# A two-layer decoder on one core: negated scores with a running minimum, one operation to mix two maps, and the gate row applied to the projection's banks

## The chip, the cores and the metric

The kernel runs on one core of a Trainium2 chip. Its engines are TensorE (PE, with its weight loads PEld), VectorE (DVE), ScalarE (ACT), GpSimd (POOL) and SyncE (SP, which issues most of the transfers). They run beside each other and wait for each other by semaphores. The metric is the device time of one execution in microseconds (us); lower is better.

## The reference

The reference is a decoder trunk of two layers on 512 tokens of 1024 channels, in float32. Cut to what matters:

```python
for l in range(2):
    sh1, sc1, g1, sh2, sc2, g2 = split(silu(c) @ w_ada[l] + b_ada[l], 6)
    h = rms(x, norm1[l]) * (1 + sc1) + sh1
    y = mlstm_mixer(h) if l == 0 else diff_attention(h)   # both end in ... @ w_out
    x = x + g1 * y
    h = rms(x, norm2[l]) * (1 + sc2) + sh2
    x = x + g2 * grouped_moe(h)        # 16 experts, 2 of 1 group of 4 for each token

def diff_attention(h):                 # 8 heads, 2 maps each, head dim 64
    q, k, v = h @ w_in                 # q, k: rms with a gain, partial rotation
    for each block of 128 queries, each head:
        sc = (q * 64**-0.5) @ k.T      # two maps c = 0, 1, causal
        p = softmax(where(mask, sc, -inf))
        o = (p[0] - lam * p[1]) @ v
    return (rms(o) * (1 - lam_init)) @ w_out
```

So the gate row `g1` (1024 values, one for each output channel) multiplies the output of the mixer's last projection.

## The kernel before

The program goes through layer 0's mixer (to about 282 us), its MoE (308 to 575), layer 1's attention (575 to 918) and its MoE (943 to the end). Between mixer and MoE lies the routing: RMS norm of each tile of 128 tokens, transposes (`x2T`, line 1075), router matmuls (`psr`, line 1087), choice and places of tokens on DVE, and an indirect transfer that gathers the tokens of each expert (`xg`, line 1311). Most matmuls of weights are done in three terms: a weight tile is split by `split` into a part `h` (ACT copy, line 228) and a remainder `l` (DVE subtraction, line 229), and `triple` (line 237) multiplies h·h, l·h and h·l.

The order on each engine is set by a scheduler that plays a timeline; a queue `later`/`step` in the kernel delays pieces of work by some steps, `ordered` keeps an instruction at its place in program order, and `tc.issue_after` holds the instructions under it behind another instruction. Tiles in PSUM come from pools of 4 (`mm`), 2 (`y`) and 2 (`t`) buffers.

**out_proj** (line 486) is the last projection of both mixers. It runs in two halves of two token tiles (t = 0, 1, then t = 2, 3); each token tile has two banks `po` of 512 columns. In half 0 the eight weight tiles `wo` (128x1024) are loaded and split, and POOL then multiplies each `wo` by the gate row `grow` in place (line 512). So half 0 needs the gate on its banks (DVE, line 499) before they are added to `x` (DVE, line 500), while half 1 splits the tiles already multiplied and only adds. The names `wos0hk` stand for layer 0, half h, weight tile k; `guse00`, `guse01` are the first tiles of the MoE's weights, split early.

**scores** (line 908) makes the two maps of a block j and a head h. For each map a matmul gives `s`, one DVE operation adds the mask row and takes the running maximum (line 920, a custom operation plus a read of its accumulator), line 923 multiplies the maximum by -0.125, and ACT takes the exponent with scale 0.125 and that bias. Then the reciprocal of the sums (line 927), the factor of map 1 (line 928), map 1 times the factor (line 929) and map 0 plus that (line 930). In `attention_constants` the column `wcq` holds the gain of q, which ACT applies when it copies the turned q (line 904).

**normed_T** (line 370) does the norm of a token tile at the start of a layer. Its `rstd_of` is a DVE operation (line 366) and a power on POOL (line 367); for t = 2, 3 of layer 1 it comes close to the last additions of layer 0's MoE (line 1616).

Of the kernel before, what the change touches and what calls it, by code (L numbers as in the profile page):

```python
# [60 lines left out]
def trunk(ctx, tc, x, c, positions, norm1, norm2, w_ada, b_ada, a_w_in, a_b_if, a_h_norm, a_w_out,  # L61
# [151 lines left out]

    loads, last, act_last = [], [], []

# [154 lines left out]
    def normed_T(l, t, pool, junk, dst, rows, bank):  # L370

        ss = small.tile([P, 1], F32, tag="ss", name=f"ss{l}{t}", bufs=4)
        A.activation(junk, xt[t], AF.Square, accum_out=ss)
        r = rstd_of(ss, 1, D, f"r{l}{t}")
        ps = [bank(f"hT{l}{t}{hf}") for hf in range(2)]
# [110 lines left out]
    def out_proj(l, half, grow, h, turned, w_out, kept, mods, done):  # L486
# [4 lines left out]
        def products(t, kt):  # L491
            while (t, kt) not in turned:
                run_first()
            triple(ps[t, 0], ps[t, 1], *(p[:, kt] for p in tokens(h, t)), *parts[kt], kt == 0, kt == NK - 1)
            if kt == NK - 1:
                for n in range(2):
                    cols = slice(n * 512, (n + 1) * 512)
                    if half == 0:
                        V.tensor_tensor(ps[t, n], ps[t, n], grow[:, cols], op=ALU.mult)
                    V.tensor_tensor(xt[t][:, cols], xt[t][:, cols], ps[t, n], op=ALU.add)  # L500
                done(t)
            step()

        for ch in range(4):
# [3 lines left out]
            for k in range(2):  # L508
                kt = ch * 2 + k
                parts[kt] = split(raw[:, k:k + 1], 1, D, f"wos{l}{half}{kt}")  # L510
                if half == 0:
                    G.tensor_tensor(raw[:, k], raw[:, k], grow, op=ALU.mult)  # L512
                if kt < NK - 3:
                    for t in ts:
                        products(t, kt)
                if k:
                    next(mods, None)
# [292 lines left out]
    def attention_constants(pool):  # L810
# [17 lines left out]
        for nm, w in (("q", b_q_norm), ("k", b_k_norm)):  # L828
# [6 lines left out]
            for c0 in (0, BHD):  # L835
                SP.dma_start(wc[c0 + R2:c0 + BHD], w[0:1, R2:].rearrange("o d -> d o"))
            tab = const.tile([P, NT, 2 * R2], F32, name=f"tab{nm}")
            bc = lambda a: a[:, None, :].to_broadcast([P, NT, ROPE_HALF])
# [9 lines left out]
    def attention(outer, mods):  # L848
# [4 lines left out]
        with ExitStack() as st:  # L853
# [12 lines left out]
            past(maskW[:, S - P:])  # L866
            V.tensor_scalar(maskW[:, S - P:], maskW[:, S - P:], 0.0, NEG, op0=ALU.is_gt, op1=ALU.mult)
            a1 = scale_of(1, slice(0, 4)) + scale_of(1, slice(4, 8))
# [39 lines left out]
            def scores(j, h):  # L908
# [5 lines left out]
                for cc in range(2):  # L914
# [4 lines left out]
                    p = pool.tile([P, S], F32, tag=f"p{cc}", name=f"p{j}{h}{cc}", bufs=3)  # L919
                    V.tensor_tensor_reduce(p[:, 0:n], ps[:, 0:n], maskW[:, S - n:S], scale=1.0, scalar=NEG,  # L920
                                           op0=ALU.add, op1=ALU.max, accum_out=mx[:, cc:cc + 1])
                    pr.append(p)
                    V.tensor_scalar(mx[:, cc:cc + 1], mx[:, cc:cc + 1], -0.125, None, op0=ALU.mult)  # L923
                    A.activation(p[:, 0:n], p[:, 0:n], AF.Exp, scale=0.125, bias=mx[:, cc:cc + 1],  # L924
                                 accum_out=mx[:, 2 + cc:3 + cc])
                p0, p1 = pr
                V.reciprocal(mx[:, 4:6], mx[:, 2:4])
                V.scalar_tensor_tensor(mx[:, 5:6], mx[:, 5:6], mx[:, 2:3], nlam, op0=ALU.mult, op1=ALU.mult)
                V.tensor_scalar(p1[:, 0:n], p1[:, 0:n], mx[:, 5:6], None, op0=ALU.mult)
                V.tensor_tensor(p0[:, 0:n], p0[:, 0:n], p1[:, 0:n], op=ALU.add)  # L930
                later(5, lambda: probs_T(j, h, p0, mx))
# [371 lines left out]
    def moe(l, pool, grow, fetch, by_rank, xgs, lst, lstd, ids, gates, rows2, twins, count, exc, past, pk, eid):  # L1303
# [269 lines left out]
        for e in range(NE):  # L1573
# [32 lines left out]
            if e == NE - 1:  # L1606
                mine = weighted_few(py, e), mine
                for t in range(NT):
# [5 lines left out]
                    for hf in range(2):  # L1614
                        x = xt[t][:, hf * 512:(hf + 1) * 512]
                        V.tensor_tensor(x, x, banks[t][hf], op=ALU.add)
            elif e >= NE - NSEL:
# [93 lines left out]
```

## Time and profile before

| | |
|---|---|
| median of 3 runs | 1228.6 us (1227.84 to 1230.41) |
| profiled execution, own time | 1225.23 us |
| its span, mean TensorE clock | 1223.4 us, 0.952 |
| PE busy | 1126.9 us (92%) |
| DVE busy | 808.9 us (66%) |
| ACT busy | 659.1 us (54%) |
| POOL busy | 307.7 us (25%) |

The span is the time from the first to the last instruction of the profiled execution. The busy shares are means over stages that have different limits. Where a row gives a clock, 1.00 is 2.4 GHz and 0.50 is 1.2 GHz; values between are means over a stretch that saw both.

### The profile page before, as it was taken

The page shows a single profiled execution, that of the slowest core. Times are in us where ns is not written, and L with a number is a line of the kernel's source. Part 1 is how long each engine was busy: PE and PEld are TensorE (multiplying, and loading weights), DVE is VectorE, ACT ScalarE, POOL GpSimd, SP SyncE. Part 2 cuts the span into 40 slices and gives each one's busy share as a digit, 9 for nine tenths or more (in the row PEclk, how much of TensorE's full clock was granted, in tenths as well). Part 3 has the DMA queues.
Part 4 walks back from the last instruction along what each step waited for, and adds up shares of the span by engine and source line. Part 5 has one row for each costly group of instructions (what it writes and reads, how often), then busy time and mean ns, then how long its engine had stood idle before and what let it go on. Part 6 is the DMA issues. An engine that isn't in the chain of part 4 may idle for free.

```text
span 1223.4 us, 17320 instructions
## 1 busy us (share of the span) xinstructions
PE 1126.9 (92%) x5954; PEld 816.0 (67%) x5954; DVE 808.9 (66%) x1617; ACT 659.1 (54%) x1118; POOL 307.7 (25%) x245
## 2 busy tenths in 40 slices
PE   5999999988999999996899999978797999999976
PEld 3677777777787875332897877757586787774322
DVE  4566878887888995006856566675677899893024
ACT  3456675443788885112655555555553888883110
POOL 2555482462211111101211021223233211111100
PEclk8999999997999999998999999988896999999998
DMA  9788662195799999999124444411275899999994
GB/s 345 267 284 302 230 216 104 59 346 194 280 383 382 386 380 368 398 408 370 37 70 141 138 169 138 173 69 74 99 280 193 316 386 385 377 380 372 396 414 182
DMA packets 104172, 320.81 MB, mean 262 GB/s; under 512 B 12673, under 2 KB 25097, under 8 KB 103056
## 3 DMA queue, kind: packets, MB, share of 16 engines
q1 hardware_dynamic: 95120, 298.67, 65.8%
q0 software_dynamic: 8960, 20.99, 4.7%
q8 instruction: 49, 0.80, 0.3%
q14 instruction: 43, 0.35, 0.1%
HBM read 309.66 MB, written 20.97 MB: 270 GB/s over the span
## 4 chain that ended last, share of the span: by engine, by line
PE 70%; DMA 12%; DVE 11%; ACT 4%; issue 2%; POOL 1%; SPq 0%; DVEq 0%; POOLq 0%; ACTq 0%
PE pge L237 8%; PE pue L237 8%; PE pge L1339 6%; PE po L237 6%; DMA we<-in_moe_w_gu_dram 5%; DMA ada<-in_w_ada_dram 5%; PE py0e L237 4%; PE py1e L237 4%; PE pye L1366 3%; PE s L917 3%; PE pcf L1398 2%; PE o L949 2%; PE xTe L427 1%; PE rowada L280 1%; PE psr L1087 1%
## 5 line engine op out<-in xcount | busy, mean ns | idle before, releaser
L1339 PE MATMUL pge<-we,xfe 128*64 128x512 f32 x448 | 106.3, 616 | 19.2 <-DMA we<-in_moe_w_gu_dram 19.2
L260 POOL TENSOR_TENSOR acc<-acc,ada 128x1024 f32<-128x1024 f32 x30 | 80.8, 2694 | 54.8 <-ACT ada L259 22.2
L1348 DVE TENSOR_TENSOR acte<-acte,pge 128x256 f32<-128x256 f32 x14 | 5.9, 421 | 119.3 <-ACT acte L1347 119.3
L1311 POOL DMA_INDIRECT xg<-h2d,lstd x26 | 26.8, 1031 | 223.0 <-PE xTe L427 152.5
L1339 PEld LDWEIGHTS pge<-we,xfe 128*64 128x64 f32 x448 | 30.4, 141 | 74.4 <-issue 51.1
L367 POOL TENSOR_TENSOR qrs<-qrs,nhalf 128x4 f32<-128x4 f32 x32 | 35.5, 1111 | 154.9 <-DVE qrs L366 126.5
L1366 PE MATMUL pye<-we,aTe 128*64 128x512 f32 x224 | 50.6, 593 | 1.1 <-ACT aTe L1355 1.1
L259 ACT ACTIVATE ada<-ada,cact 128x1024 f32<-128x1024 f32 x30 | 33.8, 1145 | 31.0 <-DMA ada<-in_w_ada_dram 31.0
L924 ACT ACTIVATE p<-p,mx 128x128 f32<-128x128 f32 (+3 forms) x64 | 35.7, 559 | 23.7 <-DVE mx L923 23.6
L920 DVE CUSTOM_DVE_ANT_0 p<-s,maskW 128x128 f32<-128x128 f32 (+3 forms) x64 | 30.4, 487 | 26.6 <-ACT orow L951 14.3
L512 POOL TENSOR_TENSOR wo<-wo,grow 128x1024 f32<-128x1024 f32 x16 | 40.9, 2573 | 23.6 <-DVE wos102l L229 15.8
L1347 ACT ACTIVATE acte<-pge 128x256 f32<-128x256 f32 x14 | 5.4, 383 | 73.1 <-PE pge L1339 73.1
L917 PE MATMUL s<-kTb,qTb 64*128 64x128 f32 (+3 forms) x128 | 40.1, 503 | 2.9 <-DVE mx L920 2.2
L1366 PEld LDWEIGHTS pye<-we,aTe 128*64 128x64 f32 x224 | 16.0, 137 | 32.3 <-issue 29.6
L427 PE MATMUL xTe<-ident,xg 128*128 128x128 f32 x144 | 23.0, 290 | 5.8 <-POOL we L220 3.2
L1463 POOL DMA_INDIRECT yd<-yoe,lstd x12 | 14.7, 1227 | 52.0 <-ACT yoe L1558 51.3
L949 PE MATMUL o<-vb,aTs 128*128 128x128 f32 x160 | 26.1, 303 | 0.7 <-ACT aTs L941 0.7
L1378 ACT ACTIVATE yo<-pye,twins 128x512 f32<-128x512 f32 x8 | 5.5, 687 | 38.9 <-PE pye L1366 38.9
L367 POOL TENSOR_TENSOR ors<-ors,nhalf 128x2 f32<-128x2 f32 (+1 forms) x12 | 11.2, 930 | 58.8 <-DVE mx L923 39.5
L949 PEld LDWEIGHTS o<-vb,aTs 128*128 128x128 f32 x160 | 23.2, 214 | 3.0 <-ACT aTs L941 1.6
L1379 POOL DMA_INDIRECT yd<-yo,rows x8 | 8.0, 1001 | 65.7 <-ACT yo L1378 65.4
L427 PEld LDWEIGHTS xTe<-ident,xg 128*128 128x128 f32 x144 | 18.5, 149 | 8.2 <-issue 6.0
(2557 smaller groups left out, 3871.5 us busy)
## 6 DMA issues: line engine op xcount, KB each, us to landing
we<-in_moe_w_gu_dram SPq DMA_DIRECT2D x128, 1024.0 KB, 8.7
we<-in_moe_w_down_dram SPq DMA_DIRECT2D x64, 1024.0 KB, 8.9
ada<-in_w_ada_dram SPq DMA_DIRECT2D x48, 1024.0 KB, 5.5
we<-yd SPq DMA_DIRECT2D x8, 1024.0 KB, 18.3
wo<-in_a_w_out_dram SPq DMA_DIRECT2D x4, 1024.0 KB, 4.9
wo<-in_b_w_out_dram SPq DMA_DIRECT2D x4, 1024.0 KB, 4.9
x<-in_x_dram SPq DMA_DIRECT2D x4, 512.0 KB, 5.0
qk0w<-in_a_w_in_dram SPq DMA_DIRECT2D x2, 1024.0 KB, 14.7
```

Source lines behind the costliest of these rows:

```text
L237: T.matmul(ps, (xh, xh, xl)[i], w, start=first and i == 0, stop=last and i == 2)
L259: A.activation(raw[:, k], raw[:, k], AF.Copy, scale=cact[:, kt:kt + 1])
L260: G.tensor_tensor(acc, acc, raw[:, k], op=ALU.add)
L367: pows.append(G.tensor_tensor(r, r, nhalf[:, 0:ncol], op=ALU.pow))
L427: T.transpose(ps[:, k * P:(k + 1) * P], row[:, kt * P:(kt + 1) * P], ident)
L512: G.tensor_tensor(raw[:, k], raw[:, k], grow, op=ALU.mult)
L917: T.matmul(ps[:, 0:n], part(qTs, h)[q0:q0 + BHD, j * P:(j + 1) * P], part(kTs, h)[q0:q0 + BHD, 0:n], start=True, stop=True)
L920: V.tensor_tensor_reduce(p[:, 0:n], ps[:, 0:n], maskW[:, S - n:S], scale=1.0, scalar=NEG, op0=ALU.add, op1=ALU.max, accum_out=mx[:, cc:cc ...
L924: A.activation(p[:, 0:n], p[:, 0:n], AF.Exp, scale=0.125, bias=mx[:, cc:cc + 1], accum_out=mx[:, 2 + cc:3 + cc])
L949: T.matmul(po[:, 0:P], aT[:, kb * P:(kb + 1) * P], part(vs, h)[:, kb * P:(kb + 1) * P], start=kb == 0, stop=kb == j)
L1339: T.matmul(pgu[hf * CS:(hf + 1) * CS].rearrange("p (g c) -> p g c", g=2), x[:, kt], w[:, :, hf], start=kt == 0, stop=kt == NK - 1))
L1366: T.matmul(py[hf * CS:(hf + 1) * CS], aT[:, k, ch * CS:(ch + 1) * CS], w[:, 0, hf * 512:(hf + 1) * 512], start=ch + k == 0, stop=ch + k == 2))
```

## The change

The score matmuls now give negated, scaled scores: `wcq` is multiplied once by -0.125, the mask row holds +1e30 where it held -1e30, line 920 takes a running minimum, and the exponent has the scale -1 with the minimum as bias, so line 923 goes. Lines 929 and 930 become one operation. In out_proj POOL's line 512 goes; both halves split the plain weight tiles and both multiply their banks by the gate row. In `normed_T` the `rstd_of` of t = 2, 3 of layer 1 is issued after the last addition of layer 0's MoE, and these additions keep the order of the program.

```diff
@@ -211,7 +211,7 @@
         G.iota(slot, pattern=[[1, P]], base=0, channel_multiplier=0, **ints)
 
 
-    loads, last, act_last = [], [], []
+    loads, last, act_last, added = [], [], [], []
 
     def load(src, a, n, name, where=None, after=None):
         pool, tag, bufs = where or (raws, "raw", N_RAW)
@@ -371,7 +371,8 @@
 
         ss = small.tile([P, 1], F32, tag="ss", name=f"ss{l}{t}", bufs=4)
         A.activation(junk, xt[t], AF.Square, accum_out=ss)
-        r = rstd_of(ss, 1, D, f"r{l}{t}")
+        with tc.issue_after(added[0].ins) if added and t > 1 else nullcontext():
+            r = rstd_of(ss, 1, D, f"r{l}{t}")
         ps = [bank(f"hT{l}{t}{hf}") for hf in range(2)]
         for kt in range(NK):
             T.transpose(ps[kt // 4][:, kt % 4 * P:(kt % 4 + 1) * P], xt[t][:, kt * P:(kt + 1) * P], ident)
@@ -495,8 +496,7 @@
             if kt == NK - 1:
                 for n in range(2):
                     cols = slice(n * 512, (n + 1) * 512)
-                    if half == 0:
-                        V.tensor_tensor(ps[t, n], ps[t, n], grow[:, cols], op=ALU.mult)
+                    V.tensor_tensor(ps[t, n], ps[t, n], grow[:, cols], op=ALU.mult)
                     V.tensor_tensor(xt[t][:, cols], xt[t][:, cols], ps[t, n], op=ALU.add)
                 done(t)
             step()
@@ -508,8 +508,6 @@
             for k in range(2):
                 kt = ch * 2 + k
                 parts[kt] = split(raw[:, k:k + 1], 1, D, f"wos{l}{half}{kt}")
-                if half == 0:
-                    G.tensor_tensor(raw[:, k], raw[:, k], grow, op=ALU.mult)
                 if kt < NK - 3:
                     for t in ts:
                         products(t, kt)
@@ -834,6 +832,8 @@
             V.memset(wc, 1.0)
             for c0 in (0, BHD):
                 SP.dma_start(wc[c0 + R2:c0 + BHD], w[0:1, R2:].rearrange("o d -> d o"))
+            if nm == "q":
+                V.tensor_scalar(wc, wc, -0.125, None, op0=ALU.mult)
             tab = const.tile([P, NT, 2 * R2], F32, name=f"tab{nm}")
             bc = lambda a: a[:, None, :].to_broadcast([P, NT, ROPE_HALF])
             V.tensor_tensor(tab[:, :, 0:8], cos, bc(wr[:, 0:8]), op=ALU.mult)
@@ -864,7 +864,7 @@
             maskW = pool.tile([P, S], F32, name="maskW")
             G.memset(maskW[:, 0:S - P], 0.0)
             past(maskW[:, S - P:])
-            V.tensor_scalar(maskW[:, S - P:], maskW[:, S - P:], 0.0, NEG, op0=ALU.is_gt, op1=ALU.mult)
+            V.tensor_scalar(maskW[:, S - P:], maskW[:, S - P:], 0.0, -NEG, op0=ALU.is_gt, op1=ALU.mult)
             a1 = scale_of(1, slice(0, 4)) + scale_of(1, slice(4, 8))
             rows = [y_tile(f"rrow1{i}") for i in range(2)]
             for t in range(NT):
@@ -917,17 +917,15 @@
                     T.matmul(ps[:, 0:n], part(qTs, h)[q0:q0 + BHD, j * P:(j + 1) * P], part(kTs, h)[q0:q0 + BHD, 0:n],
                              start=True, stop=True)
                     p = pool.tile([P, S], F32, tag=f"p{cc}", name=f"p{j}{h}{cc}", bufs=3)
-                    V.tensor_tensor_reduce(p[:, 0:n], ps[:, 0:n], maskW[:, S - n:S], scale=1.0, scalar=NEG,
-                                           op0=ALU.add, op1=ALU.max, accum_out=mx[:, cc:cc + 1])
+                    V.tensor_tensor_reduce(p[:, 0:n], ps[:, 0:n], maskW[:, S - n:S], scale=1.0, scalar=-NEG,
+                                           op0=ALU.add, op1=ALU.min, accum_out=mx[:, cc:cc + 1])
                     pr.append(p)
-                    V.tensor_scalar(mx[:, cc:cc + 1], mx[:, cc:cc + 1], -0.125, None, op0=ALU.mult)
-                    A.activation(p[:, 0:n], p[:, 0:n], AF.Exp, scale=0.125, bias=mx[:, cc:cc + 1],
+                    A.activation(p[:, 0:n], p[:, 0:n], AF.Exp, scale=-1.0, bias=mx[:, cc:cc + 1],
                                  accum_out=mx[:, 2 + cc:3 + cc])
                 p0, p1 = pr
                 V.reciprocal(mx[:, 4:6], mx[:, 2:4])
                 V.scalar_tensor_tensor(mx[:, 5:6], mx[:, 5:6], mx[:, 2:3], nlam, op0=ALU.mult, op1=ALU.mult)
-                V.tensor_scalar(p1[:, 0:n], p1[:, 0:n], mx[:, 5:6], None, op0=ALU.mult)
-                V.tensor_tensor(p0[:, 0:n], p0[:, 0:n], p1[:, 0:n], op=ALU.add)
+                V.scalar_tensor_tensor(p0[:, 0:n], p1[:, 0:n], mx[:, 5:6], p0[:, 0:n], op0=ALU.mult, op1=ALU.add)
                 later(5, lambda: probs_T(j, h, p0, mx))
 
             def probs_T(j, h, p0, mx):
@@ -1613,7 +1611,8 @@
                     to_tokens(banks[t], t, *mine, False, True)
                     for hf in range(2):
                         x = xt[t][:, hf * 512:(hf + 1) * 512]
-                        V.tensor_tensor(x, x, banks[t][hf], op=ALU.add)
+                        added[:] = [V.tensor_tensor(x, x, banks[t][hf], op=ALU.add)]
+                        ordered(added[0])
             elif e >= NE - NSEL:
                 selected.append((weighted_few(py, e), places(e)))
             elif e == NE - NSEL - 1:
```

After the change POOL's order holds 222 rows where it held 230. Around layer 1's out_proj it stands so before (`qrs` and `ors` are small powers for norms, `h` is the router's input):

```order
L367 TENSOR_TENSOR qrs<-qrs,nhalf 128x4
L512 TENSOR_TENSOR wo_8075<-wo_8075,grow_8058 128x1024 x2
L367 TENSOR_TENSOR ors_8189<-ors_8189,nhalf 128x2
L512 TENSOR_TENSOR wo_8224<-wo_8224,grow_8058 128x1024 x2
L512 TENSOR_TENSOR wo_8359<-wo_8359,grow_8058 128x1024 x2
L367 TENSOR_TENSOR ors_8286<-ors_8286,nhalf 128x2
L512 TENSOR_TENSOR wo_8390<-wo_8390,grow_8058 128x1024 x2
L367 TENSOR_TENSOR ors_8470<-ors_8470,nhalf 128x2
```

The same stretch after the change:

```order
L367 TENSOR_TENSOR qrs<-qrs,nhalf 128x4
L367 TENSOR_TENSOR ors_8107<-ors_8107,nhalf 128x2
L367 TENSOR_TENSOR ors_8199<-ors_8199,nhalf 128x2
L367 TENSOR_TENSOR ors_8366<-ors_8366,nhalf 128x2
L367 TENSOR_TENSOR ors_8375<-ors_8375,nhalf 128x2
L367 TENSOR_TENSOR ors_8455<-ors_8455,nhalf 128x2
```

All sixteen multiplications of `wo` are gone and the small powers stand directly behind each other; nothing else on POOL moves at these places.

On DVE the end of layer 1's out_proj stands so before (`x_86` and `x_89` are the token tiles t = 2 and 3, two banks each; the last row is the first of the routing behind them):

```order
L229 TENSOR_TENSOR guse00l<-we_8626,guse00h 128x1024
L500 TENSOR_TENSOR x_86<-x_86,po_8712 128x512
L500 TENSOR_TENSOR x_86<-x_86,po_8713 128x512
L500 TENSOR_TENSOR x_89<-x_89,po_8714 128x512
L229 TENSOR_TENSOR guse01l<-we_8626,guse01h 128x1024
L500 TENSOR_TENSOR x_89<-x_89,po_8715 128x512
L1138 TENSOR_TENSOR tmp_8969<-psp_8963,oh 128x64
```

The same place after:

```order
L229 TENSOR_TENSOR guse00l<-we_8519,guse00h 128x1024
L499 TENSOR_TENSOR po_8605<-po_8605,grow_7983 128x512
L499 TENSOR_TENSOR po_8606<-po_8606,grow_7983 128x512
L500 TENSOR_TENSOR x_86<-x_86,po_8605 128x512
L499 TENSOR_TENSOR po_8607<-po_8607,grow_7983 128x512
L229 TENSOR_TENSOR guse01l<-we_8519,guse01h 128x1024
L499 TENSOR_TENSOR po_8608<-po_8608,grow_7983 128x512
L500 TENSOR_TENSOR x_86<-x_86,po_8606 128x512
L500 TENSOR_TENSOR x_89<-x_89,po_8607 128x512
L500 TENSOR_TENSOR x_89<-x_89,po_8608 128x512
```

Four multiplications have come in, and the scheduler has put three of them and one addition ahead of the split of `guse01`, and the addition of the second bank of t = 2 behind it. Layer 0 has the same rows at its own end of out_proj.

The third place is on DVE in layer 1, where the scores of the last heads run beside half 0 of out_proj. Before (`mx` holds a block's maxima and sums, `p` its maps):

```order
L229 TENSOR_TENSOR wos107l<-wo_8390,wos107h 128x1024
L927 RECIPROCAL mx_8312<-mx_8312 128x2
L928 SCALAR_TENSOR_TENSOR mx_8312<-mx_8312,nlam 128x1
L929 TENSOR_SCALAR p_8321<-p_8321,mx_8312 128x128
L930 TENSOR_TENSOR p_8315<-p_8315,p_8321 128x128
L920 ISA p_8438,mx_8429<-s_8436,maskW 128x512
```

After:

```order
L926 RECIPROCAL mx_8222<-mx_8222 128x2
L927 SCALAR_TENSOR_TENSOR mx_8222<-mx_8222,nlam 128x1
L229 TENSOR_TENSOR wos107l<-wo_8294,wos107h 128x1024
L928 SCALAR_TENSOR_TENSOR p_8225<-p_8230,mx_8222,p_8225 128x128
L920 ISA p_8339,mx_8331<-s_8337,maskW 128x512
```

The pair of lines 929 and 930 is one row, and the split of `wos107` has gone from ahead of the reciprocal to just ahead of that row.

## Rows read from the trace of the kernel before

**Rows 1.** Busy time by stretch: from:to, length, each engine, PEclk, DMA share, GB/s.
```profile
600.00:808.00 208.00, 207.17 (x1531) 169.52 (x1530) 132.20 (x501) 111.36 (x304) 39.50 (x37) 1.00 0.39 132
932.00:952.00 20.00, 13.27 (x66) 11.12 (x65) 14.19 (x67) 6.26 (x8) 4.74 (x4) 0.64 0.22 75
952.00:1100.00 148.00, 147.46 (x679) 117.14 (x678) 134.07 (x134) 125.22 (x146) 21.40 (x18) 1.00 1.00 376
```

**Rows 2.** POOL in order of time, around the out_proj stages of both layers.
```profile
234.03 21.09 POOL L512 TENSOR_TENSOR wo<-wo,grow 128x1024 f32<-128x1024 f32 x8 [1.21 <-ACT grow L361]
...
814.11 5.24 POOL L512 TENSOR_TENSOR wo<-wo,grow 128x1024 f32<-128x1024 f32 x2
```

**Rows 3.** DVE in order of time, layer 0: start, us, line, operation.
```profile
237.43 2.85 DVE L727 TENSOR_TENSOR hrow<-hrow,core 128x512 f32<-128x512 f32 x1
...
243.51 0.68 DVE L302 TENSOR_REDUCE cs<-psada 128x4 f32<-128x512 f32 x1
```

**Rows 4.** What PE waited for from 230 to 262.
```profile
PE psrow L360 <- DVE swr L1030: 3.7, 1, 3.7
PE ht L427 <- DVE cs L302: 2.1, 1, 2.1
PE po L237 <- DVE wos010l L229: 0.7, 1, 0.7
```

**Rows 5.** DVE in order of time, layer 1, first place.
```profile
814.59 2.56 DVE L891 TENSOR_TENSOR qrow<-qrow,qrs 128x256 f32<-128x256 f32 x1
...
817.19 2.21 DVE L894 TENSOR_TENSOR rot<-qrow,tabk 128x32 f32<-128x32 f32 x1
819.32 0.18 DVE L895 TENSOR_TENSOR rot<-qrow,tabk 128x32 f32<-128x32 f32 x1
```

**Rows 6.** What PE waited for from 812 to 822.
```profile
PE qkT L903 <- DVE mx L928: 4.7, 1, 4.7
```

**Rows 7.** DVE in order of time, layer 1, second place.
```profile
856.57 2.19 DVE L964 TENSOR_TENSOR orow<-orow,ors 128x256 f32<-128x256 f32 x1
...
860.60 2.40 DVE L928 SCALAR_TENSOR_TENSOR mx<-mx,nlam 128x1 f32<-128x1 f32 x1
```

**Rows 8.** What PE waited for from 856 to 866.
```profile
PE s L917 <- DVE mx L920: 2.2, 1, 2.2
PE aT L939 <- ACT o L978: 2.0, 1, 2.0
```

**Rows 9.** Busy time by stretch, columns as in Rows 1.
```profile
816.00:820.00 4.00, 0.00 (x0) 0.00 (x0) 3.97 (x8) 0.49 (x2) 3.35 (x2) 0.59 0.00 0
864.00:872.00 8.00, 7.32 (x21) 4.17 (x21) 3.84 (x18) 5.12 (x19) 0.00 (x0) 0.57 0.02 5
```

**Rows 10.** DVE in order of time, end of layer 1's out_proj.
```profile
918.75 1.88 DVE L500 TENSOR_TENSOR x<-x,po 128x512 f32<-128x512 f32 x3 [0.59 <-PE po L237]
```

**Rows 11.** PE in order of time, routing of layer 0.
```profile
286.26 1.09 PE L1075 MATMUL x2T<-ident,x 128*128 128x128 f32 x8 [1.49 <-DVE x L500]
...
287.35 3.31 PE L1087 MATMUL psr<-awr,x2T 128*128 128x16 f32 x16
```

**Rows 12.** PE in order of time, routing of layer 1.
```profile
922.55 1.09 PE L1075 MATMUL x2T<-ident,x 128*128 128x128 f32 x8 [1.51 <-DVE x L500]
923.48 0.96 PE L1087 MATMUL psr<-awr,x2T 128*128 128x16 f32 x8
...
924.34 1.04 PE L1087 MATMUL psr<-awr,x2T 128*128 128x16 f32 x8
```

**Rows 13.** DVE in order of time, start of layer 1.
```profile
582.22 0.15 DVE L366 TENSOR_SCALAR r<-ss 128x1 f32<-128x1 f32 x1 [1.27 <-ACT sq L373]
```

**Rows 14.** DVE groups by line and shape: busy us, mean ns.
```profile
L923 DVE TENSOR_SCALAR mx<-mx 128x1 f32<-128x1 f32 x64 | 8.4, 147 | 0.3
...
L930 DVE TENSOR_TENSOR p<-p,p 128x512 f32<-128x512 f32 x8 | 5.5, 690 | 0.1
...
L929 DVE TENSOR_SCALAR p<-p,mx 128x512 f32<-128x512 f32 x8 | 3.9, 485 | 0.2
```

## The prediction

> **What bounds the kernel now.** I first read the page's busy shares (the table above: PE 92%) and then the busy time by stretch, since the stages have different limits. From 600 to 808 us, where attention's projections and most scores run, PE is busy 207.17 of 208.00 us at full clock: nothing that DVE saves there can shorten it. In the MoEs PE and the transfers are both full (952 to 1100: PE 147.46 of 148.00, DMA share 1.00), but in the 20 us before that the DMA share is 0.22: the transfers are not what the second MoE's start waits for, so a MoE that begins earlier ends earlier by as much [rows 1]. What is left to win or lose lies in the two out_proj stages and the routing behind them. There I read DVE in order of time, then what PE waited for, then the clock.
>
> Line 512 is sixteen POOL operations. Layer 0's eight run without a pause from 234.03 to 255.12 us, 2.64 each; two of layer 1 from 814.11 to 819.35 [rows 2]. Beside them DVE's operations with SBUF inputs grow: `hrow` takes 2.85 us, while line 302, which reads as many columns from PSUM, takes 0.68 in the same stretch [rows 3]. In layer 1 the same shows at two places: `qrow` 2.56 and `rot` 2.21, where the next `rot` of the same shape, after POOL has ended, takes 0.18 [rows 5]; then `orow` 2.19 and the factor `mx`, one column, 2.40 [rows 7]. PE waits for exactly these: 3.7 + 2.1 + 0.7 = 6.5 us in layer 0 [rows 4], 4.7 us at the first place in layer 1 [rows 6], 2.2 + 2.0 = 4.2 us at the second [rows 8].
>
> It isn't the weights' transfers that slow DVE: from 816 to 820 the DMA share is 0.00, and DVE is busy 3.97 of 4.00 us while PE does nothing [rows 9].
>
> The Trainium skill says this in "SBUF — State Buffer", section "Who interferes with whom": a DVE operation with two SBUF inputs and a GpSimd operation that reads SBUF exclude each other for the whole instruction. The rows above agree, down to the PSUM operand that is spared.
>
> **The change, part by part.**
>
> *Line 512 goes, layer 0.* DVE's order at this place stays as it was, so the stretched operations shrink where they stand and PE's three waits go: +6.5 us. Something on DVE still stands between (two operations of line 302, four tiny ones), so the lower end is 5.5; the clock, which sinks while PE waits, could give 1.0 back: 5.5 to 7.5.
>
> *Line 512 goes, layer 1, first place.* The chain through `qrow`, `rot`, `mx` to `qkT` loses 4.7 us of waiting [rows 6]. On that chain stand also one line 923 (0.15) and one line 929 of 512 columns (0.49) [rows 14], of which the chain keeps nothing: I count +0.3 for them, since ACT's exponent runs beside. +5.0. Behind it ACT and DVE pass the outputs of attention to each other with two buffers; if that becomes the later chain at once, 1 us of it is lost: 4.0 to 6.5 (upper end: PE's next microseconds also at full clock).
>
> *Layer 1, second place.* PE's 4.2 us go, and then the clock: from 864 to 872 PE is busy 7.32 of 8.00 us at a mean grant of 0.57, that is mostly at 1.2 GHz after its idle time [rows 9]. Without the idle time before it the same work at 2.4 GHz would take up to 0.43 of 7.32 us less, 3.1; I take two thirds of it, +2.0. Together +6.2, between 3.5 (no clock, something else late by 0.7) and 7.3.
>
> *The gate on the banks of half 1.* Four more of line 499 in each layer, at the very end of out_proj, where PE has nothing else. Three additions of the same shape take 1.88 us, so one more operation costs 0.60 in a row [rows 10]. The split of `guse01` stays among them, now with three multiplications ahead of it. The first of these rows starts when PE releases its bank, as before; so the last addition comes 4 x 0.60 = 2.4 us later, and behind it wait the transposes `x2T`, the router, the choice, the gather and the MoE. Layer 0: -2.4 (2.0 to 3.5). The router's matmuls of layer 0 are already at the low clock (16 in 3.31 us [rows 11]) and can't fall further.
>
> Layer 1 is different. There the same sixteen took 0.96 + 1.04 us at the high clock [rows 12], after PE had idled 1.51 us; in layer 0, after 1.49 us, they were slow. [...] After the change `x2T` of t = 2 waits too, because the addition of its second bank now stands behind `guse01`: of the 1.51 + 2.40 = 3.9 us that PE will then idle ahead of `x2T` of t = 3, nearly all lies in one piece. I take these sixteen at layer 0's price, 3.31 for 2.00: -1.3 more. Layer 1: -3.7 (2.4 to 5.0, the lower clock reaching the transposes).
>
> The Trainium skill, "TensorE: Matmul & The Clock Gate", section "What's actually happening", speaks against the change here: the throttled state is the default and only activity releases it, so that a longer gap costs clock as well as time. By the rule the term is -3.7, by layer 1's own row alone -2.4.
>
> *Line 923 goes, lines 929 and 930 become one.* 64 operations of 0.147 us, 8.4 us of DVE, and 32 of line 929 (0.485 at 512 columns). The new operation has two SBUF inputs and no row before; its price lies between line 930's 0.690 at 512 columns and the sum of both, 1.175; I take 0.69, since line 930 reads and writes the same tiles [rows 14]. Nearly all of this lies in 600 to 808, where PE covers it [rows 1]: 0. Without that cover a block of 512 columns would save 0.485 and, by two of line 923, 0.29. If the running minimum were slower than the maximum, PE would cover the first 0.1 or so; it is the same operation with another comparison, and I take equal. The operation on `wcq` is one column, 0.15 at line 923's price; it runs in layer 0's first stage, far from its use, hidden; 0.15 if it weren't.
>
> *The order at the start of layer 1.* DVE stood 1.27 us for ACT at `r` of t = 2 and held the last additions back [rows 13]. These now come first, so the square sum of t = 3 begins that much earlier; its power and transposes follow, and I count +0.8 of it (0 to 1.0), the rest being ACT's and POOL's own time.
>
> **Sum.** 6.5 - 2.4 + 0.8 + 5.0 + 6.2 - 3.7 = +12.4 us, by the ends from +4.5 (5.5 - 3.5 + 0 + 4.0 + 3.5 - 5.0) to +17.9 (7.5 - 2.0 + 1.0 + 6.5 + 7.3 - 2.4). The profiled execution took 1225.23 us, so 1212.8; the median of the runs shown lies 3.4 above it, so 1216.2 in terms of the median. I forecast 1216.
>
> **Rivals.**
>
> *Half of it is swallowed (0.22).* At both places of layer 1 the chain goes through ACT's copies too. If these are the later chain once DVE is fast, a wait for ACT takes the place of each wait for DVE, and only layer 0's 6.5 and about half of 9.0 stay: 6.5 + 4.5 - 2.4 - 3.7 = +4.9, so 1223.7. For it: PE's 2.0 at `aT` is written down to ACT's `o` [rows 8]. Against: that `o` was itself late by the rows that POOL stretched.
>
> *More clock than counted (0.10).* Without the gaps PE stays at 2.4 GHz through the rest of out_proj, and the tail doesn't lose it: the upper end, 1210.7.
>
> *Slower (0.07).* DVE's long rows come from something that stays (POOL's small powers, the splits' ACT half), and the waits stay with them. Then only the tails are left: -2.4 - 3.7 + 0.8 = -5.3, so 1233.9. It decides once less than 5.3 of the 15.7 us of PE's waits go. Against: `rot` ends at 819.40, as line 512 does, and the next of its shape is twelve times shorter [rows 2, 5].
>
> *No change (0.06).* What goes just pays for the tails, 1226 to 1231. That the change doesn't do what it says is excluded for line 512, which is gone from POOL's order; the scheduler's other moves are small.
>
> **Numbers.** The forecast itself has 0.55: 1212 to 1220. The range takes in the swallowed case and the upper end, and some 2 us for the profiled execution against the median: 1208 to 1226. A measurement here tells 0.2%, 2.5 us, from no change; faster by more than that has 0.55 + 0.22 + 0.10 = 0.87, none 0.06, slower 0.07.
>
> **What would show it.** Right: no DVE row of one operation above 1.4 us in both out_proj stages; PE's waits for `swr`, `cs` and `mx` gone; lines 499 and 500 as a run of eight with `guse01` at the end, `x2T` waiting 3 us or more, and the sixteen `psr` of layer 1 near 3.3 us. Wrong: long DVE rows that stay without line 512; new PE waits of 2 us and more for ACT's `o`, `orow` or the `wos` copies; a gather that comes later than 2.4 us after the last matmul of out_proj by more than now; or a MoE that begins 12 us earlier and doesn't end so.

## The result and the profile after

The changed kernel took 1213.48 us (median of 4 runs, 1211.09 to 1217.86) beside 1229.47 us for the kernel before: ratio 0.9875, 95% interval 0.9844 to 0.9907. Timed once more (`changed_again`, below) it was 1219.53 us (6 runs) beside 1230.51: 0.9899, 0.9867 to 0.9931. So it is 11 to 16 us faster, where +12.4 was forecast.

The profiled execution took 1217.86 us (span 1216.1), 4.4 above the median of the first four runs, while that of before lay 3.4 below its own. The difference of the two spans is therefore a poor measure, and I compare stages. Part of what lies between executions arises ahead of out_proj, where the order on the engines is the same. There POOL's line 260 adds up rows of 1024 columns and reads two operands from SBUF, as line 512 does. In the changed kernel's profile the weights' remainder `v1s2` came 2.9 us after POOL had begun a run of three such additions; it took 3.42 us, and PE waited for it:

```profile
141.20 8.53 POOL L260 TENSOR_TENSOR acc<-acc,ada 128x1024 f32<-128x1024 f32 x3 [4.12 <-ACT ada L259]
144.09 3.42 DVE L229 TENSOR_TENSOR v1s2l<-v1w,v1s2h 128x1024 fp32r<-128x1024 f32 x1
147.56 0.50 PE L456 MATMUL v1p<-v1s2l,ah 128*128 128x512 f32 x1 [2.43 <-DVE v1s2l L229]
```

In a later kernel with the same order there (`tail_late`, below) the same remainder began 0.06 us ahead of POOL's addition and took 1.21 us:

```profile
140.77 1.21 DVE L229 TENSOR_TENSOR v1s2l<-v1w,v1s2h 128x1024 fp32r<-128x1024 f32 x1
140.83 6.28 POOL L260 TENSOR_TENSOR acc<-acc,ada 128x1024 f32<-128x1024 f32 x2 [0.53 <-ACT ada L259]
```

The granted clock from 140 to 150 us was 0.92 in the one and 1.00 in the other. The first matmul of out_proj (`wos000h`) begins at 215.30 us in the one and at 210.00 in the other; in the kernel before it was 211.94, and in the second profile of the changed kernel 216.29. The table takes stages from there on, from the start or end of the named matmuls in the order of time on PE, in us; each column is one execution. `gate_only`, `scores_only`, `tail_late` and `changed_again`, the changed kernel a second time, are experiments below. `bv6s0h` is a late weight tile of layer 1's projections; both places of layer 1 lie behind it.

| stage | before | changed | changed_again | gate_only | scores_only | tail_late |
|---|---|---|---|---|---|---|
| layer 0, half 0: first `wos000` to last `wos007` | 42.10 | 34.53 | 34.53 | 34.53 | 46.94 | 34.54 |
| layer 0, half 1: to last `wos017` | 29.79 | 28.60 | 28.61 | 28.61 | 29.34 | 28.60 |
| routing: to first `xTe` | 24.48 | 28.25 | 27.72 | 27.46 | 22.80 | 25.61 |
| MoE's first weights: to first `guse10h` | 14.20 | 15.23 | 16.58 | 15.18 | 14.45 | 14.28 |
| layer 1's mixer: first `b00s0h` to last `wos117` | 331.85 | 319.28 | 321.92 | 318.89 | 328.86 | 320.86 |
| of it, to first `bv6s0h` | 200.48 | 203.26 | 205.89 | 200.93 | 203.02 | 201.48 |
| of it, from there on | 131.37 | 116.03 | 116.03 | 117.96 | 125.85 | 119.38 |
| routing: to first `xTe` | 23.12 | 27.44 | 27.35 | 28.18 | 22.62 | 25.10 |
| MoE's first weights: to first `guse10h` | 14.17 | 15.30 | 15.32 | 16.35 | 14.62 | 16.62 |

Won: 7.57 + 1.19 in layer 0's out_proj, 12.57 in layer 1's mixer, which is 15.34 won behind `bv6s0h` and 2.78 lost ahead of it. The second profile has the same 15.34, but 5.41 lost ahead of it. What is lost there goes with a lower clock (mean grant 0.991 before, 0.975 and 0.967 in the two profiles of the changed kernel). Given back: 3.77 + 1.03 and 4.32 + 1.13 behind the two out_proj stages.

DVE in layer 0. Beside [rows 3] the two pairs of `a` and the remainder of `wos010` are further long ones in the kernel before:

```profile
245.88 2.37 DVE L398 TENSOR_SCALAR a<-mod 128x4 f32<-128x4 f32 x2
...
248.77 1.78 DVE L399 TENSOR_TENSOR a<-a,vcol 128x4 f32<-128x4 f32 x2
...
252.95 3.25 DVE L229 TENSOR_TENSOR wos010l<-wo,wos010h 128x1024 fp32r<-128x1024 f32 x1
```

The changed kernel:

```profile
239.14 0.69 DVE L725 TENSOR_TENSOR hrow<-hrow,core 128x512 f32<-128x512 f32 x1
...
242.86 0.24 DVE L399 TENSOR_SCALAR a<-mod 128x4 f32<-128x4 f32 x2
...
243.61 0.22 DVE L400 TENSOR_TENSOR a<-a,vcol 128x4 f32<-128x4 f32 x2
...
248.79 1.22 DVE L229 TENSOR_TENSOR wos010l<-wo,wos010h 128x1024 fp32r<-128x1024 f32 x1
...
255.52 2.30 DVE L1091 SCALAR_TENSOR_TENSOR h<-h,re,srow 128x1024 f32<-128x1024 f32 x1 [0.73 <-POOL h L1065]
...
259.59 2.29 DVE L229 TENSOR_TENSOR wos012l<-wo,wos012h 128x1024 fp32r<-128x1024 f32 x1 [1.12 <-PE po L237]
```

`hrow` takes 0.69 where it took 2.85, the pairs 0.24 and 0.22, the remainder 1.22. Long rows have not gone altogether: the last two stand beside POOL's work on the router's input (line 1065), which stays and also reads SBUF; PE doesn't wait for them. PE's waits of [rows 4] are gone without a successor: from 230 to 262 us the view lists none, and PE is full at full clock. A stretch before and after (columns as in [rows 1]):

```profile
252.00:256.00 4.00, 3.59 (x19) 2.80 (x17) 4.00 (x3) 1.99 (x3) 4.00 (x3) 0.81 1.02 406
```

```profile
252.00:256.00 4.00, 4.00 (x23) 3.37 (x22) 3.27 (x7) 2.56 (x6) 2.32 (x3) 1.00 1.03 411
```

DVE in layer 1, the rows that answer to [rows 5, 7]:

```profile
814.97 0.42 DVE L891 TENSOR_TENSOR qrow<-qrow,qrs 128x256 f32<-128x256 f32 x1
...
815.90 0.19 DVE L894 TENSOR_TENSOR rot<-qrow,tabk 128x32 f32<-128x32 f32 x1
...
849.63 0.42 DVE L962 TENSOR_TENSOR orow<-orow,ors 128x256 f32<-128x256 f32 x1
...
853.83 0.22 DVE L927 SCALAR_TENSOR_TENSOR mx<-mx,nlam 128x1 f32<-128x1 f32 x1
```

What PE waited for in layer 1, 800 to 905 us (total, times, longest; the first three):

```profile
PE oT L974 <- ACT o L976: 3.8, 3, 1.5
PE po L237 <- ACT o2h L979: 1.8, 2, 1.2
PE o L947 <- ACT aTs L939: 1.2, 3, 0.5
```

The waits for `mx` of [rows 6, 8] and the one for `o` at `aT` are gone. The three for `o` at `oT` were there before (3.9); the one for `o2h` grew from 1.2 to 1.8, that for `aTs` from 0.7 to 1.2.

The end of layer 1's out_proj, on DVE:

```profile
905.76 1.30 DVE L499 TENSOR_TENSOR po<-po,grow 128x512 f32<-128x512 f32 x2 [0.59 <-PE po L237]
906.97 0.68 DVE L500 TENSOR_TENSOR x<-x,po 128x512 f32<-128x512 f32 x1
907.56 0.69 DVE L499 TENSOR_TENSOR po<-po,grow 128x512 f32<-128x512 f32 x1
908.16 1.91 DVE L229 TENSOR_TENSOR guse01l<-we,guse01h 128x1024 fp32r<-128x1024 f32 x1
910.00 0.69 DVE L499 TENSOR_TENSOR po<-po,grow 128x512 f32<-128x512 f32 x1
910.60 1.87 DVE L500 TENSOR_TENSOR x<-x,po 128x512 f32<-128x512 f32 x3
```

Beside [rows 10], the four multiplications have come in as the order showed. But the split of `guse01` takes 1.91 us where it took 1.35: POOL works on the router's input beside it, from 907.73 to 908.99. The kernel before:

```profile
920.55 1.35 DVE L229 TENSOR_TENSOR guse01l<-we,guse01h 128x1024 fp32r<-128x1024 f32 x1
```

On PE the same place after the change, in answer to [rows 12]:

```profile
907.70 0.66 PE L1073 MATMUL x2T<-ident,x 128*128 128x128 f32 x4 [0.57 <-DVE x L500]
911.32 1.12 PE L1073 MATMUL x2T<-ident,x 128*128 128x128 f32 x4 [2.97 <-DVE x L500]
...
914.28 1.73 PE L1085 MATMUL psr<-awr,x2T 128*128 128x16 f32 x8
...
916.33 1.87 PE L1085 MATMUL psr<-awr,x2T 128*128 128x16 f32 x8
```

The transposes of t = 2 come in two pieces with 2.97 us of idle time between, and the sixteen `psr` take 1.73 + 1.87 where they took 2.00. The clock by stretch:

```profile
907.00:911.00 4.00, 0.79 (x5) 0.42 (x4) 4.00 (x6) 1.06 (x1) 1.26 (x1) 0.83 0.78 247
911.00:914.00 3.00, 2.67 (x14) 2.52 (x15) 2.88 (x9) 2.67 (x5) 1.08 (x2) 0.50 1.02 408
914.00:918.00 4.00, 4.00 (x23) 4.00 (x22) 3.93 (x10) 1.69 (x4) 3.06 (x3) 0.50 0.65 255
```

It fell to 0.50 from 911 on; before, it held to 926.

At the start of layer 1, in answer to [rows 13], `r` of t = 2 no longer waits (1.27 before). `r` of t = 3 waited 0.86 before and waits 1.08 now; it begins 0.41 us earlier, while the additions ahead of it begin at the same time (576.45 and 576.49). The kernel before, then the changed one:

```profile
584.86 0.15 DVE L366 TENSOR_SCALAR r<-ss 128x1 f32<-128x1 f32 x1 [0.86 <-ACT sq L373]
```

```profile
584.45 0.15 DVE L366 TENSOR_SCALAR r<-ss 128x1 f32<-128x1 f32 x1 [1.08 <-ACT sq L373]
```

The new mixing operation and the running minimum, by line and shape (busy us, mean ns, then idle time before):

```profile
L920 DVE CUSTOM_DVE_ANT_0 p<-s,maskW 128x512 f32<-128x512 f32 x16 | 10.9, 688 | 8.1 <-PE s L917 5.7 <-ACT orow L949 2.3
...
L928 DVE SCALAR_TENSOR_TENSOR p<-p,mx,p 128x512 f32<-128x512 f32 x8 | 6.0, 748 | 0.2
```

The mixing of 512 columns takes 0.748, near line 930's 0.690 [rows 14] and far from the 1.175 of the pair. The minimum takes what the maximum took (688 ns at 512 columns in both kernels).

### The profile page after: what moved, and what is told of

Read it like the earlier page. It is cut to its first block, busy times and chain, and to the rows that moved or that the text cites. A ratio compares the mean times of both kernels' runs of the same rounds, so it can differ in the third digit from the quotient of the medians.

```text
span 1216.1 us, 17193 instructions
## 1 busy us (share of the span) xinstructions
PE 1129.1 (93%) x5954; PEld 818.1 (67%) x5954; DVE 780.0 (64%) x1530; ACT 658.1 (54%) x1118; POOL 264.3 (22%) x229
## 4 chain that ended last, share of the span: by engine, by line
PE 76%; DMA 11%; DVE 5%; ACT 3%; POOL 3%; issue 1%; SPq 0%; DVEq 0%; POOLq 0%; ACTq 0%
PE pge L237 8%; PE pue L237 8%; PE po L237 7%; PE pge L1337 6%; DMA we<-in_moe_w_gu_dram 5%; PE py0e L237 4%; PE py1e L237 4%; DMA ada<-in_w_ada_dram 4%; PE pye L1364 3%; PE s L917 2%; POOL acc L260 2%; PE pcf L1396 2%; PE psr L1085 2%; PE xTe L428 1%; PE o L947 1%; PE rowada L280 1%
## 5 line engine op out<-in xcount | busy, mean ns | idle before, releaser
L888 DVE TENSOR_REDUCE qss<-qsq 128x4 f32<-128x256 f32 x32 | 13.2, 415 | 16.9 <-ACT qsq L887 16.5
L949 ACT ACTIVATE orow<-o,mx 128x128 f32<-128x128 f32 x32 | 11.3, 363 | 23.2 <-PE o L947 23.2
```

## Experiments

Two theories. **The stretch:** line 512's reads on POOL hold up DVE's operations with SBUF inputs, PE waits for these, and removing line 512 gives all the gain. **Less work:** DVE has 29 us less to do (808.9 to 780.0), and that is the gain. A third asks whether the gain came from half 1 no longer waiting for multiplied weights.

**gate_only**: the kernel before with the gate's part alone.

```diff
-                    if half == 0:
-                        V.tensor_tensor(ps[t, n], ps[t, n], grow[:, cols], op=ALU.mult)
+                    V.tensor_tensor(ps[t, n], ps[t, n], grow[:, cols], op=ALU.mult)
...
-                if half == 0:
-                    G.tensor_tensor(raw[:, k], raw[:, k], grow, op=ALU.mult)
```

> The kernel before with the gate's part alone: line 512 gone, both halves multiply their banks. If the gain comes from DVE's operations no longer being held up by POOL, this part alone gives nearly all of the 16 us: a median 12 to 18 us below the kernel before. If it comes from the scores' shorter work on DVE, it gives under 5 us, or costs up to 6 by the four multiplications at each end of out_proj.

Measured 1218.4 us (6 runs), ratio 0.9907 (0.9878 to 0.9937): 8 to 15 us faster than the kernel before. Its stages are close to those of the changed kernel, layer 1's mixer too: 13.41 us are won behind `bv6s0h` (131.37 - 117.96). Most of the gain or all of it.

**scores_only**: the kernel before with the scores' part alone.

```diff
-                                           op0=ALU.add, op1=ALU.max, accum_out=mx[:, cc:cc + 1])
+                                           op0=ALU.add, op1=ALU.min, accum_out=mx[:, cc:cc + 1])
...
-                    V.tensor_scalar(mx[:, cc:cc + 1], mx[:, cc:cc + 1], -0.125, None, op0=ALU.mult)
...
-                V.tensor_scalar(p1[:, 0:n], p1[:, 0:n], mx[:, 5:6], None, op0=ALU.mult)
-                V.tensor_tensor(p0[:, 0:n], p0[:, 0:n], p1[:, 0:n], op=ALU.add)
+                V.scalar_tensor_tensor(p0[:, 0:n], p1[:, 0:n], mx[:, 5:6], p0[:, 0:n], op0=ALU.mult, op1=ALU.add)
```

> The kernel before with the scores' part alone: negated scores, running minimum, one operation to mix; line 512 stays. By the first theory within 2.5 us of the kernel before, since PE is busy all the time where most scores run; DVE is some 20 us less busy. By the second theory 5 to 16 us faster.

Measured 1226.78 us (12 runs, 1217.34 to 1228.96), ratio 0.9957 (0.993 to 0.9984): 2 to 9 us faster. That is more than nothing, so the first theory is not the whole of it: with line 512 still there the scores' part wins 5.52 us behind `bv6s0h` (131.37 - 125.85), where `order_only`, with the scores as before, takes 131.29. Why isn't shown: at the first place `qrow` and `rot` are as long as before (2.48 and 2.12). The two parts don't simply add. With the gate's part already in, the scores' part is worth 0.9 to 1.5 us from `bv6s0h` to the first `wos107` (78.55 in `gate_only`, 77.06 to 77.66 in the eight profiles that have both parts); behind that these nine take 38.97 to 42.10 us, `gate_only` 39.41. Its profiled execution shows something else, in layer 0's out_proj, where its DVE rows stand in the order of the kernel before:

```profile
244.62 4.59 DVE L398 TENSOR_SCALAR a<-mod 128x4 f32<-128x4 f32 x2
...
249.73 4.07 DVE L399 TENSOR_TENSOR a<-a,vcol 128x4 f32<-128x4 f32 x2
```

```profile
PE psrow L360 <- DVE swr L1030: 8.2, 1, 8.2
```

The same four small operations took 2.37 and 1.78 before and take 4.59 and 4.07 here, and PE's wait for `swr` grows from 3.7 to 8.2. `order_only`, the third profile with this order, has 2.37 and 1.78 again. So the order alone doesn't set how long DVE is held up by the same POOL work.

**order_only**: the kernel before with the held-back `rstd_of` and the ordered additions.

```diff
-        r = rstd_of(ss, 1, D, f"r{l}{t}")
+        with tc.issue_after(added[0].ins) if added and t > 1 else nullcontext():
+            r = rstd_of(ss, 1, D, f"r{l}{t}")
...
-                        V.tensor_tensor(x, x, banks[t][hf], op=ALU.add)
+                        added[:] = [V.tensor_tensor(x, x, banks[t][hf], op=ALU.add)]
+                        ordered(added[0])
```

> The kernel before with the order at the start of layer 1 alone: the power for t = 2, 3 issued behind the last additions. The prediction counted 0.8 us; by the profile after it is nothing or a loss of 0.5. Either way within 2.5 us of the kernel before.

Measured 1229.99 us (12 runs), ratio 1.0006 (0.9983 to 1.0028): no difference that shows. The interval reaches from 2 us faster to 3 us slower, so it can't tell the forecast 0.8 us from nothing. **no_order** is the changed kernel without these lines.

> The changed kernel without the order at the start of layer 1. That part alone made no difference to the kernel before, so within 3 us of the changed kernel. If it matters only once the rest is fast, 1 to 3 us slower than it.

Measured 1217.63 us (6 runs), beside 1219.53 for the changed kernel in the same rounds (0.9901, 0.9872 to 0.993, beside 0.9899): no difference that shows either.

**gate_twice**: the changed kernel with another operation on the banks of half 1.

```diff
                     V.tensor_tensor(ps[t, n], ps[t, n], grow[:, cols], op=ALU.mult)
+                    if half:
+                        V.tensor_scalar(ps[t, n], ps[t, n], 1.0, None, op0=ALU.mult)
```

> The changed kernel with one more operation on each bank of half 1 (a multiplication by 1.0 behind the gate, which leaves the result as it is): four more at the end of out_proj in each layer. If what stands there lies on the path to the routing, each layer pays 4 x 0.60 = 2.4 us or more and the clock besides: 5 to 9 us slower than the changed kernel, so 7 to 11 us below the kernel before. If the gathers' or the weights' own time covers it, no difference to the changed kernel.

Measured 1222.91 us (9 runs), ratio 0.9943 (0.9917 to 0.9969), against 0.9875 and 0.9899 of the changed kernel: by the ratios some 5 to 8 us slower than it, by the medians 3.4 (1219.53); its interval overlaps the second of the two. PE's wait for the last additions, in layer 0:

```profile
PE x2T L1075 <- DVE x L502: 4.8, 2, 4.1
```

It was 3.5, with 3.0 the longest. The routing takes 29.44 and 28.36 us, 1.2 to 1.7 and 0.9 to 1.0 more than in the changed kernel's two profiles. What stands at the end of out_proj is on the path, though this profile shows less than the 2.4 us for each layer that four operations take on DVE.

**pool_read**: the changed kernel with POOL's products put back in layer 0, into a tile that nobody needs yet.

```diff
...
+                if l == 0 and half == 0:
+                    held_up[:] = [G.tensor_tensor(scr[0], raw[:, k], grow, op=ALU.mult)]
...
```

The router's input of t = 0, 1 on POOL is held behind the last of them, as it stood before.

> The changed kernel with POOL's eight multiplications of wo by the gate row put back in layer 0 alone, written to a tile that nobody needs yet; the order of DVE there is that of the changed kernel, and nothing waits for these products but POOL's own later work. If it is POOL's reading beside DVE that stretches DVE, the long DVE rows (2.4 to 3.4 us) come back between 230 and 256 us, PE waits 6 us or more there, and the time goes up by 7 to 10 us against the changed kernel. If the gain came from half 1 no longer waiting for multiplied weights, nothing changes: within 3 us of the changed kernel.

**pool_write**: the same with POOL only writing.

```diff
...
+                if l == 0 and half == 0:
+                    for w in (D, D, 512):
+                        held_up[:] = [G.memset(scr[0][:, 0:w], 0.0)]
...
```

> As the kernel with POOL's products put back in layer 0, but POOL fills the same tile with zeros (2560 columns for each weight tile), so it is as long busy there and only writes. If POOL's reads are what DVE waits for, DVE's rows stay short (1.2 us for a weight's remainder) and the time is that of the changed kernel within 3 us. If any work on POOL stretches DVE, or if a busy POOL delays its powers, it is 7 to 10 us slower, as with the products.

With the products 1230.1 us (12 runs), ratio 1.0 (0.9978 to 1.0022): all of the gain gone, by layer 0 alone; layer 1's mixer keeps its gain (320.36 us). With the zeros 1218.71 us (6 runs), 0.9925 (0.9899 to 0.9951): by the ratios 3 to 6 us above the changed kernel, whose intervals it overlaps, by the medians no slower (1219.53). So the expected "within 3 us" of it is not quite shown for the whole kernel. In both, POOL began them only at 241 to 242 us, behind a release by PE, so half 1 bears them: it takes 39.12 us with the products and 29.92 with the zeros, against 28.60. That is another place than in the kernel before, where line 512 lay beside half 0. DVE with the products, two of the remainders of half 1's first four weights (the other two take 3.19 and 2.58):

```profile
249.29 2.22 DVE L229 TENSOR_TENSOR wos011l<-wo,wos011h 128x1024 fp32r<-128x1024 f32 x1
...
260.47 3.41 DVE L229 TENSOR_TENSOR wos013l<-wo,wos013h 128x1024 fp32r<-128x1024 f32 x1
```

DVE with the zeros (the other two take 1.22 and 1.23), and POOL beside it up to 262 us:

```profile
246.22 1.22 DVE L229 TENSOR_TENSOR wos011l<-wo,wos011h 128x1024 fp32r<-128x1024 f32 x1
...
256.35 1.23 DVE L229 TENSOR_TENSOR wos013l<-wo,wos013h 128x1024 fp32r<-128x1024 f32 x1 [0.43 <-PE po L237]
```

```profile
241.10 7.76 POOL L513 MEMSET xg<- 128x1024 f32 x9 [9.83 <-PE ht L428]
...
252.33 9.78 POOL L513 MEMSET xg<- 128x1024 f32 x11
```

The same four operations in the same order take 2.22 to 3.41 us beside a POOL that reads two operands from SBUF, and 1.22 to 1.23 beside a POOL that is about as busy (242.21 to 266.10 us with the products, 241.10 to 262.69 with the zeros) and only writes. In the views no wait of DVE or PE there is put down to the products. So in layer 0 it is neither the dependence of half 1 on multiplied weights nor a busy POOL, but POOL's reading. For layer 1 this is inferred: `gate_only` shows that line 512 is what matters there, and [rows 5, 7] show the same lengthening, of operations that don't touch the tiles that POOL reads. The rule of the Trainium skill that the prediction named ("SBUF — State Buffer", section "Who interferes with whom") says that a GpSimd operation that only writes doesn't hold up such a DVE operation; these rows agree.

**tail_order** takes up the price of the tail: t = 2 is finished before t = 3, and the split of `guse01` stands behind the last addition.

```diff
+                    with tc.issue_after(tail[0].ins) if t == 3 else nullcontext():
+                        V.tensor_tensor(ps[t, n], ps[t, n], grow[:, cols], op=ALU.mult)
...
+        with tc.issue_after(tail[0].ins):
+            ready.append(split(fetch.ready[0][:, 1:2], 1, D, "guse01"))
```

> The changed kernel with another order at the end of out_proj's half 1: both banks of t = 2 are multiplied and added before those of t = 3, and the split of guse01 stands behind the last addition. If the split of 1.9 us among the multiplications lies on the path, each layer's routing begins about 1.9 us earlier and PE's gap before the transposes falls from 3.0 to some 1.5: 3 to 6 us faster than the changed kernel. If DVE's later work there only moves (the split then delays the choice of places), within 2 us of it.

Measured 1217.47 us (6 runs), 0.9901 (0.9876 to 0.9926): no gain. PE in layer 0's routing, and DVE there:

```profile
277.23 1.29 PE L1076 MATMUL x2T<-ident,x 128*128 128x128 f32 x8
...
282.81 0.40 PE L1146 MATMUL psl<-told,hot 128*128 128x32 f32 x1 [4.26 <-DVE hot L1145]
```

```profile
277.66 1.22 DVE L229 TENSOR_TENSOR guse01l<-we,guse01h 128x1024 fp32r<-128x1024 f32 x1
...
280.04 2.27 DVE L1094 SCALAR_TENSOR_TENSOR xg<-xg,re,srow 128x1024 f32<-128x1024 f32 x1 [0.93 <-POOL xg L1068]
...
282.47 2.05 DVE L1145 TENSOR_SCALAR hot<-slot,pk 128x128 fp32r<-128x128 f32 x4
```

The transposes of t = 3 begin 3.05 us after the last matmul of out_proj (277.23 - 274.18), where the changed kernel needed 5.40 (283.83 - 278.43). But then PE waits 4.26 us for `hot`: DVE first does the split and an operation on the router's input that POOL's reads stretch to 2.27, and PE's order has `psl` ahead of `psr`.

**tail_late**: as before, but the split stands behind the last such operation (line 1091 of the changed kernel) of t = 3.

> The changed kernel with t = 2 finished before t = 3 at the end of out_proj's half 1, as in the first try, and the split of guse01 behind the last row of the routing's input (line 1091 of t = 3). In the first try PE then waited 4.3 us for the columns of `hot` on DVE, behind the split and a stretched operation. If that wait was what swallowed the 2.3 us by which the last transposes came earlier, layer 0's gather comes 2 us earlier now and the kernel is 2 to 5 us faster than the changed one. If the low clock in the routing eats it, within 2 us.

Measured 1213.71 us (6 runs, 1210.22 to 1215.73), ratio 0.9869 (0.9841 to 0.9896), beside 1219.53 and 0.9899 for the changed kernel in the same rounds. The intervals overlap, and the changed kernel's first measurement was 0.9875, so that it beats the changed kernel is not certain. PE in layer 0's routing:

```profile
276.19 1.28 PE L1076 MATMUL x2T<-ident,x 128*128 128x128 f32 x8
...
278.13 0.30 PE L1146 MATMUL psl<-told,hot 128*128 128x32 f32 x1 [0.61 <-DVE hot L1145]
278.27 3.58 PE L1088 MATMUL psr<-awr,x2T 128*128 128x16 f32 x16
```

The wait for `hot` is 0.61, and the routing takes 25.61 us in layer 0 and 25.10 in layer 1, where the changed kernel took 28.25 and 27.44 (27.72 and 27.35 in its second profile).

**changed_again** is the changed kernel itself.

> The changed kernel itself, once more, on the chip and in the rounds of the two kernels beside it, since single executions of it spread over 7 us. By the prediction 8 to 18 us below the kernel before; the gate's part and the scores' part, timed alone, add up to some 12 to 16.

Measured 1219.53 us (6 runs, 1213.21 to 1221.68), as told above. The two parts alone would make 1 - 0.0093 - 0.0043 = 0.9864; 0.9875 and 0.9899 lie there or a little short of it.

## Why the prediction was right, step by step

The sign, the cause and the sum were right. The terms were too small on both sides, and that the sum met the measurement is in part luck: 8.8 + 15.3 us were won at the three places where 6.5 + 5.0 + 6.2 were forecast, 10.3 were lost in the tails where 6.1 were forecast, and 2.8 to 5.4 were lost ahead of `bv6s0h`, for which nothing was forecast.

- *Layer 0 without line 512*, forecast +6.5 (5.5 to 7.5): the stages gave 7.57 + 1.19 = 8.8, above the upper end. PE's waits were read rightly and came back whole; the term was short by the clock, which had been 0.76 and 0.81 from 248 to 256 us and is now 1.00, and by half 1, which the term didn't cover.
- *Layer 1, both places*, +5.0 and +6.2: the stretch that holds them became 15.3 us shorter in both profiles of the changed kernel, above the sum of the upper ends (13.8). The mechanism was right, with the long rows and PE's waits for them gone and the mean granted clock of the stretch up from 0.883 to 0.956; the size was too small. 13.4 of it came with the gate's part alone. New waits for ACT, the rival of the swallowed half, came to 0.6 at `o2h` and 0.5 at `aTs`.
- *The tails*, -2.4 and -3.7: 3.77 + 1.03 and 4.32 + 1.13, so -4.8 and -5.5; the second profile has -5.6 and -5.4. The count of 4 x 0.60 held. What was missing: `guse01`'s split, which stood between two additions and now has multiplications on both sides, is itself stretched by POOL's work for the router (1.35 to 1.91), and the lower clock reached further in both layers, to the first weights of the MoE (mean grant 0.89 before; 0.82 and 0.81 after in layers 0 and 1). The prediction held that layer 0's router couldn't fall further; its matmuls couldn't, but the transposes ahead of them (1.97 us for the eight of t = 3, 1.09 before [rows 11]) and the MoE's first ones did. Of the two values weighed for layer 1's clock, the one by which a longer gap costs clock held: 2.97 us of idle time, then 0.50. The Trainium skill's rule that the throttled state is the default ("TensorE: Matmul & The Clock Gate", "What's actually happening") agrees with it.
- *The start of layer 1*, +0.8: at DVE 0.4 of it is seen in one profile; whether the kernel gains it stays open, since `order_only` can't resolve it.
- *The scores' part*, +0.3 at the first place and 0 where PE is full: with the gate's part in place it is worth 0.9 to 1.5 us up to `wos107`. Without it, it gives 2 to 9 us, which the sum had no term for: the prediction priced the parts as if each stood on its own. Whether it costs something in the stretch ahead of `bv6s0h` isn't shown: the three profiles without it take 200.5 to 200.9 us there, the nine with it 200.9 to 205.9.
- *The rival of slower*, that DVE's long rows come from something that stays, is refuted by the rows after the change, by pool_read and by pool_write. PE's waits that it weighs add up to 15.4 us (6.5 + 4.7 + 4.2), not 15.7.

Of the signs, PE's waits for `swr`, `cs` and `mx` went, `x2T` waits 3.5 us, and the sixteen `psr` of layer 1 take 3.60. Three came out otherwise. DVE rows above 1.4 us stay beside POOL's work for the router (2.30 and 2.29 above), off PE's path. `guse01` stands inside the run of eight, as the order after the change already showed. And the routing grew by 3.8 and 4.3 us, more than the 2.4 that the prediction named as a sign of being wrong; what was wrong there is the size of the tails.

By the stages the sum is 8.8 - 4.8 + 12.6 - 5.5 = 11.1, and from the first `wos000h` to the last `pcf` it is 9.7 ((1217.34 - 211.94) - (1210.99 - 215.30)), the two MoEs taking 0.2 and 1.2 more; the second profile gives 7.2 ((1217.34 - 211.94) - (1214.51 - 216.29)). The medians say 11 to 16, the forecast was 12.4. The kernel before was profiled in an execution faster than its median and the changed one twice in a slower one, so the profiles understate the gain; how much of it lies ahead of out_proj isn't shown.

## What to carry to other kernels

An operation that is moved off a busy engine isn't free because its new engine idles: look at the rows of the engine beside it, and compare the same shape with and without that neighbour. Here the four operations at the very end of a stage cost their 2.4 us of DVE time and the clock behind it, so a multiplication there was dearer than one in the middle. If a stage's tail is shortened, read the order behind it too: the next operation in the queue can take the whole gain, as the first of the two tries did.

## What was not expected of the hardware

How long DVE is held up by POOL is not a property of the order alone: with the same rows in the same order, two small operations took 2.37 us in two profiles and 4.59 in a third, and the next two 1.78, 1.78 and 4.07. The same holds ahead of out_proj, where POOL's line 260 also reads two operands: one remainder took 3.42 us in one execution and 1.21 in another, in which it began 0.06 us ahead of POOL. Such waits and a lower clock near them let two kernels that are equal up to there begin out_proj 5 us apart. The clock alone doesn't set it: `pool_read` had 0.83 from 84 to 92 us, lower than the changed kernel's 0.90, and began out_proj at 211.47. None of this can be read off one profile; what decides between a gate row on one engine or another has to be compared by stage.
